# Residual add and layer norm: sums moved to GpSimd, and transfers of 16 rows split into even and odd partitions

## The chip, the cores and the metric

The kernel runs on one core of a Trainium2 chip. A core has five engines that run side by side: TensorE (PE, matrix products), VectorE (DVE), ScalarE (ACT), GpSimd (POOL) and SyncE (SP), which here only issues transfers. Sixteen DMA engines move data between the chip's memory (HBM) and the on-chip buffer SBUF (128 partitions). PSUM is a second, small on-chip buffer of eight banks, into which TensorE writes its results. The metric is device time in microseconds (us), the median of several runs; smaller is better.

## The reference

Input are `x` and `residual`, both 16 x 1024 x 512 in fp32, and `gamma` and `beta` of 512 elements. Each of the 16384 rows is normalized by itself:

```python
z = x + residual
mean = np.mean(z, axis=-1, keepdims=True)
var = np.var(z, axis=-1, keepdims=True)
z_norm = (z - mean) / np.sqrt(var + eps)
return (gamma * z_norm + beta).astype(np.float32)
```

The two inputs are 33.5 MB each, and so is the output: 100.7 MB cross the DMA engines.

## The kernel before

**Tiling.** The 16384 rows are laid over 128 partitions, so each partition has 128 rows of 512 elements; "row j" below means one such row in every partition, a tile of 128x512. `dram` (L58) cuts the input and output in blocks of the store sizes (`OUT_CHUNKS`: seven of 16 rows, then 8, 4, 4); in a block a partition owns as many neighbouring rows of HBM as the block has, so a 16-row store is one run of 32 KB per partition and an 8-row load one run of 16 KB.

**Buffers.** `zbuf` holds 64 rows of x, which become the sum, then the result, in place. `rbuf` holds 32 rows of the residual. Both are rings.

**Transfers.** All are issued by SyncE, in the order in which the last loop of the kernel asks for them: 8 rows of x (L81), 8 rows of the residual (L84), and a store (L87) when `STORE_LAG` = 40 rows more have been asked for than the store's last row. SyncE's queue is in order: a transfer that must wait holds back all behind it. A load of x waits until the store of the rows whose place it takes has landed. A load of the residual waits until the sums of the rows 32 before it are done. A store waits until its rows are finished. The DMA engines serve the issued transfers in order.

**Compute.** It goes by groups of four rows. A group passes through these stages, in three successive steps, so that three groups are under way at once:

1. `add` (L132, L133): TensorE multiplies the row of x, then the row of the residual, by an identity matrix into one PSUM bank, which adds them. Of every eight rows the last is left to VectorE (`add_on_vector`, L140).
2. `copy_then_sqrt` (L156): ScalarE copies the sum from PSUM to `zbuf` and gives the row's total; it also takes the root of the variance of an older group (L197). `negmean` (L171): VectorE turns the totals into negative means.
3. `square` (L185): ScalarE squares the centred row into a scratch tile in SBUF, for the sum of squares.
4. `affine1` (L209): VectorE adds the negative mean and multiplies by gamma. `affine2` (L222, L224): it takes the reciprocal of the root, multiplies by it and adds beta. Both work in place.

Gamma and beta are spread over the partitions at the start by a product with a column of ones (`spread`, L115) and copied to SBUF (L116). The program writes the order of the work on each engine out by hand (`manual_schedule`); the framework only adds the waits.

Of the kernel before, what the change touches and what calls it, by code (L numbers as in the profile page):

```python
# [7 lines left out]

FP32 = mybir.dt.float32
ACT = mybir.ActivationFunctionType  # L10
ALU = mybir.AluOpType

X_CHUNKS = [8] * 15 + [4, 4]
R_CHUNKS = [8] * 15 + [4, 4]
OUT_CHUNKS = [16] * 7 + [8, 4, 4]

GROUP = 4

Z_ROWS = 64
R_ROWS = 32

STORE_LAG = 40

ADD_PERIOD = 8


@with_exitstack
def kernel(  # L30
# [9 lines left out]
    nc = tc.nc  # L40
    P = nc.NUM_PARTITIONS
    xf = x.flatten_outer_dims()
    rf = residual.flatten_outer_dims()
    of = out.flatten_outer_dims()
    N, D = xf.shape
    inv_d = 1.0 / float(D)
    total = N // P

    def spans(sizes):

        assert sum(sizes) == total
        return [(sum(sizes[:c]), n) for c, n in enumerate(sizes)]

    blocks = spans(OUT_CHUNKS)

    def dram(t, lo, n):  # L58

        b0, bn = next(b for b in blocks if b[0] <= lo and lo + n <= b[0] + b[1])  # L60
        v = t[P * b0 : P * (b0 + bn), :].rearrange("(p j) d -> p j d", p=P)
        return v[:, lo - b0 : lo - b0 + n, :].rearrange("p a b -> p (a b)")

    consts = ctx.enter_context(tc.tile_pool(name="consts", bufs=1))
    small = ctx.enter_context(tc.tile_pool(name="small", bufs=6))
    junkp = ctx.enter_context(tc.tile_pool(name="junkp", bufs=2))
    psum = ctx.enter_context(
        tc.tile_pool(name="psum", bufs=8, space=bass.MemoryType.PSUM)
    )
    ctx.enter_context(tc.manual_schedule())  # L70

# [1 line left out]
    zbuf = consts.tile([P, Z_ROWS, D], FP32)  # L73
    rbuf = consts.tile([P, R_ROWS, D], FP32)

    def part(buf, size, lo, n):
        assert lo % size + n <= size
        return buf[:, lo % size : lo % size + n, :].rearrange("p a b -> p (a b)")

    def load_x(lo, n):  # L80
        nc.sync.dma_start(out=part(zbuf, Z_ROWS, lo, n), in_=dram(xf, lo, n))  # L81

    def load_r(lo, n):
        nc.sync.dma_start(out=part(rbuf, R_ROWS, lo, n), in_=dram(rf, lo, n))  # L84

    def store(lo, n):
        nc.sync.dma_start(out=dram(of, lo, n), in_=part(zbuf, Z_ROWS, lo, n))  # L87

    def zrow(j):
        return zbuf[:, j % Z_ROWS, :]  # L90

    def rrow(j):
        return rbuf[:, j % R_ROWS, :]

    def on_vector(j):
        return j % ADD_PERIOD == ADD_PERIOD - 1

    gb_row = consts.tile([1, 2, D], FP32)  # L100
    nc.scalar.dma_start(out=gb_row[:, 0, :], in_=gamma[None, :])
    nc.scalar.dma_start(out=gb_row[:, 1, :], in_=beta[None, :])
    ones = consts.tile([1, P], FP32)
    nc.vector.memset(ones, 1.0)  # L104
    eps_t = consts.tile([P, 1], FP32)
    nc.vector.memset(eps_t, float(eps))
    ident = consts.tile([P, P], FP32)
    make_identity(nc, ident)
    gamma_t = consts.tile([P, D], FP32)
    beta_t = consts.tile([P, D], FP32)  # L110

    def spread():
        for k, dest in ((0, gamma_t), (1, beta_t)):
            ps = psum.tile([P, D], FP32, tag="ps", name="ps")
            nc.tensor.matmul(ps, ones, gb_row[:, k, :], start=True, stop=True)  # L115
            nc.vector.tensor_copy(dest, ps)  # L116

    groups = []
    for lo, n in spans(R_CHUNKS):
        for j in range(0, n, GROUP):  # L120
            groups.append((lo + j, min(GROUP, n - j)))
    n_groups = len(groups)
    PS, SM, NM, SSQ, STD = {}, {}, {}, {}, {}

    def add(g):
        j0, n = groups[g]
        SM[g] = small.tile([P, GROUP], FP32, tag="sm", name="sm")
        for j in range(j0, j0 + n):
            if on_vector(j):
                continue  # L130
            ps = psum.tile([P, D], FP32, tag="ps", name="ps")
            nc.tensor.matmul(ps, ident, zrow(j), start=True, stop=False)  # L132
            nc.tensor.matmul(ps, ident, rrow(j), start=False, stop=True)  # L133
            PS[j] = ps

    def add_on_vector(g):
        j0, n = groups[g]
        for j in range(j0, j0 + n):
            if on_vector(j):
                nc.vector.scalar_tensor_tensor(  # L140
                    out=zrow(j),
                    in0=zrow(j),
                    scalar=0.0,
                    in1=rrow(j),
                    op0=ALU.add,
                    op1=ALU.add,
                    accum_out=SM[g][:, j - j0 : j - j0 + 1],
                )

    def copy_then_sqrt(g):  # L150

        j0, n = groups[g] if g < n_groups else (0, 0)
        before = g - 2 if g >= 2 else None
        for j in range(j0, j0 + n):
            if j in PS:
                nc.scalar.activation(  # L156
                    out=zrow(j),
                    in_=PS.pop(j),
                    func=ACT.Identity,
                    accum_out=SM[g][:, j - j0 : j - j0 + 1],  # L160
                )
                if before is not None:
                    sqrt(before)
                    before = None
        if before is not None:
            sqrt(before)

    def negmean(g):
        n = groups[g][1]
        nm = small.tile([P, GROUP], FP32, tag="nm", name="nm")  # L170
        nc.vector.tensor_scalar(  # L171
            out=nm[:, :n],
            in0=SM.pop(g)[:, :n],
            scalar1=-inv_d,
            scalar2=None,
            op0=ALU.mult,
        )
        NM[g] = nm

    def square(g):  # L180
        j0, n = groups[g]
        ssq = small.tile([P, GROUP], FP32, tag="ssq", name="ssq")
        for k in range(n):
            junk = junkp.tile([P, D], FP32, tag="junk", name="junk")
            nc.scalar.activation(  # L185
                out=junk,
                in_=zrow(j0 + k),
                func=ACT.Square,
                bias=NM[g][:, k : k + 1],
                accum_out=ssq[:, k : k + 1],  # L190
            )
        SSQ[g] = ssq

    def sqrt(g):
        n = groups[g][1]
        std = small.tile([P, GROUP], FP32, tag="std", name="std")
        nc.scalar.activation(  # L197
            out=std[:, :n],
            in_=SSQ.pop(g)[:, :n],
            func=ACT.Sqrt,  # L200
            bias=eps_t[:, 0:1],
            scale=inv_d,
        )
        STD[g] = std

    def affine1(g):
        j0, n = groups[g]
        for k in range(n):
            nc.vector.scalar_tensor_tensor(  # L209
                out=zrow(j0 + k),  # L210
                in0=zrow(j0 + k),
                scalar=NM[g][:, k : k + 1],
                in1=gamma_t,
                op0=ALU.add,
                op1=ALU.mult,
            )
        NM.pop(g)

    def affine2(g):
        j0, n = groups[g]  # L220
        rstd = small.tile([P, GROUP], FP32, tag="rstd", name="rstd")
        nc.vector.reciprocal(out=rstd[:, :n], in_=STD.pop(g)[:, :n])  # L222
        for k in range(n):
            nc.vector.scalar_tensor_tensor(  # L224
                out=zrow(j0 + k),
                in0=zrow(j0 + k),
                scalar=rstd[:, k : k + 1],
                in1=beta_t,
                op0=ALU.mult,
                op1=ALU.add,  # L230
            )

    def compute_steps():

        stages = [
            (0, add),
            (0, copy_then_sqrt),
            (1, square),
            (2, affine2),
            (0, add_on_vector),  # L240
            (1, affine1),
            (0, negmean),
        ]
        added = done = 0
        for t in range(n_groups + 2):
            for lag, stage in stages:
                if 0 <= t - lag < n_groups or stage is copy_then_sqrt:
                    stage(t - lag)
            if t < n_groups:
                added += groups[t][1]  # L250
            if t >= 2:
                done += groups[t - 2][1]
            yield added, done

    steps = compute_steps()
    added = done = asked = 0
    loads_r = spans(R_CHUNKS)
    stores = spans(OUT_CHUNKS)
# [10 lines left out]

    for lo, n in spans(X_CHUNKS):  # L270
        asked = lo + n
        assert not stores or stores[0][0] >= asked - Z_ROWS
        load_x(lo, n)
        while loads_r and loads_r[0][0] + loads_r[0][1] <= asked:

            while added < loads_r[0][0] + loads_r[0][1] - R_ROWS:
                added, done = next(steps)
# [39 lines left out]
```

## Time and profile before

| | |
|---|---|
| Median of 10 runs | 242.79 us (242.38 to 243.36) |
| The profiled execution's own time | 243.22 us |
| Its span (first to last instruction) | 241.3 us |
| TensorE matmul busy | 203.3 us (84%) |
| VectorE busy | 192.7 us (80%) |
| ScalarE busy | 169.9 us (70%) |
| GpSimd busy | 0.7 us |
| Moved | 100.79 MB, 418 GB/s on average |

How to read it: "busy" is the time in which an engine runs at least one instruction, and says nothing of whether it is waited for. A page has the busy share of every engine in 40 equal slices of the span, as tenths; a 9 means 90% or more. The row of DMA is the mean over the 16 DMA engines. A group line gives the source line, engine, operation, output and inputs, shape, count, busy time in all and the mean of one in nanoseconds. A timeline line gives start and duration in us, then engine, line and operation; "x4" means four in a row. SPq is SyncE's queue, in which the issue of a transfer appears; the transfer itself is in the DMA rows. "q1" is the queue of the loads and stores, "q8" and "q14" are queues on which instructions are fetched.

### The profile page before, as it was taken

Reading aid. Unit: us, or ns where it says so; the run is one execution under the profiler, and the core shown is the slowest. Engines: PE = TensorE matmul, PEld = TensorE weight load, DVE = VectorE, ACT = ScalarE, POOL = GpSimd, SP = SyncE. Lnnn points to the kernel's source line nnn. Section 1 sums busy time; section 2 is a strip of 40 time slices with the busy share of each in tenths; the row PEclk is TensorE's granted clock in tenths of the full one; section 3 lists DMA queues with packets and bytes.
Section 4 is the critical chain, followed back from the end, with each engine's and each line's share of the span. In section 5 each row is a group of like instructions: output and inputs, shape, how many; then the busy total and the mean of one; then the engine's idle time right before and its main releaser. Section 6 shows DMA issues by size and latency. Waiting matters only on the chain.

```text
span 241.3 us, 1990 instructions
## 1 busy us (share of the span) xinstructions
PE 203.3 (84%) x452; PEld 87.6 (36%) x452; DVE 192.7 (80%) x356; ACT 169.9 (70%) x514; POOL 0.7 (0%) x6
## 2 busy tenths in 40 slices
PE   3689999999999999999999996899959999891000
PEld 0134444444444444444444442344414444340000
DVE  1101279999999999999999999739997699989940
ACT  0213699797979797979797979269783888786500
POOL 1000000000000000000000000000000000000000
PEclk9999999999999999999999999799999999997555
DMA  7999999999999999999999999999999999999993
GB/s 261 435 435 435 432 427 424 417 427 431 435 465 435 388 428 421 435 429 427 428 432 437 436 424 429 424 451 418 416 432 432 469 391 414 462 426 435 410 414 148
DMA packets 6351, 100.79 MB, mean 418 GB/s; under 512 B 706, under 2 KB 706, under 8 KB 708
## 3 DMA queue, kind: packets, MB, share of 16 engines
q1 hardware_dynamic: 6336, 100.67, 98.0%
q8 instruction: 4, 0.07, 0.1%
q14 instruction: 7, 0.06, 0.1%
q10 hardware_dynamic: 4, 0.00, 0.0%
HBM read 67.11 MB, written 33.55 MB: 417 GB/s over the span
## 4 chain that ended last, share of the span: by engine, by line
PE 53%; DMA 34%; DVE 7%; SPq 1%; ACT 1%; issue 0%; DVEq 0%
DMA rbuf<-in_residual_dram 34%; PE ps L133 27%; PE ps L132 26%; DVE zbuf L209 3%; DVE zbuf L224 3%; SPq L81 0%; ACT junk L185 0%; ACT zbuf L156 0%; DVEq L312 0%; DVE zbuf L140 0%; SPq L87 0%; DVE rstd L222 0%; SPq L84 0%; DVE nm L171 0%; DVEq L209 0%
## 5 line engine op out<-in xcount | busy, mean ns | idle before, releaser
L133 PE MATMUL ps<-rbuf,ident 128*128 128x512 f32 x224 | 117.5, 607 | 9.9 <-DMA rbuf<-in_residual_dram 6.7
L132 PE MATMUL ps<-zbuf,ident 128*128 128x512 f32 x224 | 117.7, 607 | 0.0
L209 DVE SCALAR_TENSOR_TENSOR zbuf<-zbuf,nm,gamma_t 128x512 f32<-128x512 f32 x128 | 89.5, 749 | 12.6 <-ACT junk L185 12.6
L156 ACT ACTIVATE zbuf<-ps 128x512 f32<-128x512 f32 x112 | 66.0, 589 | 46.9 <-PE ps L133 46.9
L185 ACT ACTIVATE junk<-zbuf,nm 128x512 f32<-128x512 f32 x128 | 90.4, 711 | 1.6 <-DVE nm L171 1.6
L224 DVE SCALAR_TENSOR_TENSOR zbuf<-zbuf,rstd,beta_t 128x512 f32<-128x512 f32 x128 | 87.7, 748 | 1.1
L133 PEld LDWEIGHTS ps<-rbuf,ident 128*128 128x128 f32 x224 | 43.0, 194 | 67.0 <-issue 53.0
L132 PEld LDWEIGHTS ps<-zbuf,ident 128*128 128x128 f32 x224 | 43.6, 195 | 56.3 <-issue 43.1
L185 ACT ACTIVATION_READ_ACCUMULATOR junk<-zbuf,nm 128x1 f32 x128 | 24.3, 190 | 0.0
L156 ACT ACTIVATION_READ_ACCUMULATOR zbuf<-ps 128x1 f32 x112 | 21.8, 195 | 0.0
L171 DVE TENSOR_SCALAR nm<-sm 128x4 f32<-128x4 f32 x32 | 5.2, 163 | 13.6 <-ACT zbuf L156 13.6
L140 DVE SCALAR_TENSOR_TENSOR zbuf<-zbuf,rbuf 128x512 f32<-128x512 f32 x16 | 11.0, 686 | 0.0
L197 ACT ACTIVATE std<-ssq,eps_t 128x4 f32<-128x4 f32 x32 | 9.3, 289 | 0.1
L222 DVE RECIPROCAL rstd<-std 128x4 f32<-128x4 f32 x32 | 5.6, 174 | 3.8 <-ACT std L197 3.8
L115 PE MATMUL ps<-gb_row,ones 1*128 1x512 f32 x4 | 4.1, 1129 | 4.6 <-DMA gb_row<-in_gamma_dram 2.4
L156 ACT ACT_TABLE_LOAD x1 | 1.3, 1283 | 8.1 <-DMA zbuf<-in_x_dram 8.1
L116 DVE COPY beta_t<-ps 128x512 f32<-128x512 f32 x1 | 0.7, 692 | 3.6 <-PE ps L115 3.6
L116 DVE COPY gamma_t<-ps 128x512 f32<-128x512 f32 x1 | 0.7, 692 | 3.5 <-PE ps L115 3.5
L115 PEld LDWEIGHTS ps<-gb_row,ones 1*128 1x128 f32 x4 | 1.0, 307 | 6.1 <-DMA gb_row<-in_beta_dram 3.8
L140 DVE DVE_READ_ACCUMULATOR zbuf<-zbuf,rbuf 128x1 f32 x16 | 1.3, 83 | 0.0
L197 ACT ACT_TABLE_LOAD x1 | 1.3, 1283 | 0.0
L104 DVE MEMSET ones<- 1x128 f32 x1 | 0.2, 165 | 0.8 <-PEq L298 0.8
(7 smaller groups left out, 1.0 us busy)
## 6 DMA issues: line engine op xcount, KB each, us to landing
zbuf<-in_x_dram SPq DMA_DIRECT2D x15, 2048.0 KB, 25.2
rbuf<-in_residual_dram SPq DMA_DIRECT2D x15, 2048.0 KB, 20.8
out_dram<-zbuf SPq DMA_DIRECT2D x7, 4096.0 KB, 28.7
zbuf<-in_x_dram SPq DMA_DIRECT2D x2, 1024.0 KB, 33.1
rbuf<-in_residual_dram SPq DMA_DIRECT2D x2, 1024.0 KB, 33.1
out_dram<-zbuf SPq DMA_DIRECT2D x1, 2048.0 KB, 15.5
out_dram<-zbuf SPq DMA_DIRECT2D x2, 1024.0 KB, 10.2
gb_row<-in_gamma_dram ACTq DMA_DIRECT2D x1, 2.0 KB
```

The source lines that it names most:

```text
L115: nc.tensor.matmul(ps, ones, gb_row[:, k, :], start=True, stop=True)
L116: nc.vector.tensor_copy(dest, ps)
L132: nc.tensor.matmul(ps, ident, zrow(j), start=True, stop=False)
L133: nc.tensor.matmul(ps, ident, rrow(j), start=False, stop=True)
L140: nc.vector.scalar_tensor_tensor(out=zrow(j), in0=zrow(j), scalar=0.0, in1=rrow(j), op0=ALU.add, op1=ALU.add, accum_out=SM[g][:, j - j0 : ...
L156: nc.scalar.activation(out=zrow(j), in_=PS.pop(j), func=ACT.Identity, accum_out=SM[g][:, j - j0 : j - j0 + 1],)
L171: nc.vector.tensor_scalar(out=nm[:, :n], in0=SM.pop(g)[:, :n], scalar1=-inv_d, scalar2=None, op0=ALU.mult,)
L185: nc.scalar.activation(out=junk, in_=zrow(j0 + k), func=ACT.Square, bias=NM[g][:, k : k + 1], accum_out=ssq[:, k : k + 1],)
L197: nc.scalar.activation(out=std[:, :n], in_=SSQ.pop(g)[:, :n], func=ACT.Sqrt, bias=eps_t[:, 0:1], scale=inv_d,)
L209: nc.vector.scalar_tensor_tensor(out=zrow(j0 + k), in0=zrow(j0 + k), scalar=NM[g][:, k : k + 1], in1=gamma_t, op0=ALU.add, op1=ALU.mult,)
L222: nc.vector.reciprocal(out=rstd[:, :n], in_=STD.pop(g)[:, :n])
L224: nc.vector.scalar_tensor_tensor(out=zrow(j0 + k), in0=zrow(j0 + k), scalar=rstd[:, k : k + 1], in1=beta_t, op0=ALU.mult, op1=ALU.add,)
```

## The change

It has two steps that come together.

First, the arithmetic is moved. GpSimd adds a whole group in one instruction, in place in `zbuf`. ScalarE runs both statistics passes from `zbuf` into scratch tiles in PSUM: an Identity with scale -1/512, whose accumulator gives the negative mean directly, then the Square, then the root, whose result is in PSUM too. TensorE only spreads gamma and beta, which stay in PSUM, where VectorE's affine instructions read them. The stages of a group are issued one after the other with no lag between groups; the table of ScalarE's root function is loaded at the start by a small instruction (`warm`).

Second, loads of x are of 16 rows, loads of the residual of 8, 8, six times 16, 8, 4, 4, and blocks in HBM are always of 16 rows. A transfer of 16 rows is issued as two, one of the even and one of the odd partitions, 2 MB each with runs of 32 KB.

```diff
-X_CHUNKS = [8] * 15 + [4, 4]
-R_CHUNKS = [8] * 15 + [4, 4]
+BLOCK = 16
+X_CHUNKS = [16] * 8
+R_CHUNKS = [8, 8] + [16] * 6 + [8, 4, 4]
 OUT_CHUNKS = [16] * 7 + [8, 4, 4]
-ADD_PERIOD = 8
...
     def dram(t, lo, n):
-        b0, bn = next(b for b in blocks if b[0] <= lo and lo + n <= b[0] + b[1])
-        v = t[P * b0 : P * (b0 + bn), :].rearrange("(p j) d -> p j d", p=P)
-        return v[:, lo - b0 : lo - b0 + n, :].rearrange("p a b -> p (a b)")
+        k = lo % BLOCK
+        v = t[P * (lo - k) : P * (lo - k + BLOCK), :].rearrange("(p j) d -> p j d", p=P)
+        return v[:, k : k + n, :].rearrange("p a b -> p (a b)")
...
+    def transfer(out, in_, n):
+        parts = 2 if n == BLOCK else 1
+        for h in range(parts):
+            nc.sync.dma_start(out=out[h::parts, :], in_=in_[h::parts, :])
     def load_x(lo, n):
-        nc.sync.dma_start(out=part(zbuf, Z_ROWS, lo, n), in_=dram(xf, lo, n))
+        transfer(part(zbuf, Z_ROWS, lo, n), dram(xf, lo, n), n)
...
     def add(g):
         j0, n = groups[g]
+        z = part(zbuf, Z_ROWS, j0, n)
+        nc.gpsimd.tensor_tensor(
+            out=z, in0=z, in1=part(rbuf, R_ROWS, j0, n), op=ALU.add
+        )
...
+    def statistics(g):
+        j0, n = groups[g]
+        nm = small.tile([P, GROUP], FP32, tag="nm", name="nm")
+        ssq = small.tile([P, GROUP], FP32, tag="ssq", name="ssq")
+        for k in range(n):
+            junk = junkp.tile([P, D], FP32, tag="junk", name="junk")
+            nc.scalar.activation(
+                out=junk,
+                in_=zrow(j0 + k),
+                func=ACT.Identity,
+                scale=-inv_d,
+                accum_out=nm[:, k : k + 1],
+            )
+        for k in range(n):
+            junk = junkp.tile([P, D], FP32, tag="junk", name="junk")
+            nc.scalar.activation(
+                out=junk,
+                in_=zrow(j0 + k),
+                func=ACT.Square,
+                bias=nm[:, k : k + 1],
+                accum_out=ssq[:, k : k + 1],
+            )
+        std = stdp.tile([P, GROUP], FP32, tag="std", name="std")
+        nc.scalar.activation(
+            out=std[:, :n],
+            in_=ssq[:, :n],
+            func=ACT.Sqrt,
+            bias=eps_t[:, 0:1],
+            scale=inv_d,
+        )
...
+    gamma_t = fixed.tile([P, D], FP32, name="gamma_t")
+    beta_t = fixed.tile([P, D], FP32, name="beta_t")
...
+        for g in range(n_groups):
+            add(g)
+            statistics(g)
+            affine1(g)
+            affine2(g)
```

`fixed`, `junkp` (three buffers) and `stdp` (three) are pools in PSUM. `affine1` and `affine2` are as before but for the place of gamma and beta. The identity matrix, `add_on_vector`, `copy_then_sqrt` and `negmean` are gone.

## The prediction

> **What bounds the kernel now.** I read the page of the profiled execution first, the busy shares and the slices before anything else.
>
> ```profile
> span 241.3 us, 1990 instructions
> PE 203.3 (84%) x452; PEld 87.6 (36%) x452; DVE 192.7 (80%) x356; ACT 169.9 (70%) x514; POOL 0.7 (0%) x6
> ...
> DMA  7999999999999999999999999999999999999993
> ...
> q1 hardware_dynamic: 6336, 100.67, 98.0%
> q8 instruction: 4, 0.07, 0.1%
> q14 instruction: 7, 0.06, 0.1%
> ```
>
> TensorE is the busiest engine and fills half of the chain that ended last, but the DMA row is full from the second slice to the last but one, and the queue of loads and stores takes 98.0% of 16 engines' span. The transfers bound this kernel; the chain runs through TensorE because matmuls follow each other while the loads wait in a full queue. The tail says the same. In the timeline of SyncE and VectorE near the end:
>
> ```profile
> 181.19 50.81 SPq L87 DMA_DIRECT2D out_dram<-zbuf  x5
> ...
> 228.90 2.74 DVE L224 SCALAR_TENSOR_TENSOR zbuf<-zbuf,rstd,beta_t 128x512 f32<-128x512 f32 x4
> ```
>
> The last arithmetic ends at 231.6, and the stores still run to 240.2. The last store (8 packets of 0.309 an engine) has its place at 237.7 and needs 1.3 from issue to first packet, so compute had nearly 5 us to spare.
>
> So I went to the trace's record of each DMA packet. The median packet of 16 KB takes 0.611 us, of 32 KB 1.213, of 8 KB 0.309; a completion write takes 0.009. Each of the 16 engines carries 248, 56 and 48 of them (3968, 896 and 768 in all): 151.5 + 67.9 + 14.8 = 234.3, with 44 completion writes 234.7. The first packet starts at 2.0, so an undisturbed engine ends at 236.7. The last completion writes of the 16 engines lie at 236.71 (the first engine), within 0.3 of that for half of them, and at 237.7 to 240.17 for the other half. The span ends 1.1 later. So the time is 2.0 + 234.7 + 3.5 (the slowest engine's lateness) + 1.1 = 241.3. The profiled execution took 243.22, 1.92 outside the span; the median of the runs is 242.79, 0.43 less.
>
> What makes an engine late? Between 45 and 52 us, while two instruction fetches run (8 KB at 45.4 in 0.31 us, 16 KB at 47.5 in 1.10), the slowest engine's lateness goes from 0.4 to 1.9. By the first store, at 71, it is 2.8, with no fetch of its own there. The four 16 KB fetches (row q8) take 1.04 us on average.
>
> **What the skill says.** "Runtime: NRT & Kernel Launch", section Instruction fetch mechanics: instructions stream in 16 KiB blocks of 256, over DMA. This agrees with row q8: TensorE's 904 instructions are 3.5 blocks, and there are four such packets. "GPSIMD Engine Reference", section Performance versus the Vector engine: an add of two fp32 tensors with 2048 elements a partition takes 4497 ns on GpSimd. No row here shows one. "SBUF — State Buffer", section Who interferes with whom: a VectorE instruction with one SBUF input, outside the two-port modes, does not contend with GpSimd, one with two SBUF inputs does. Before, GpSimd is idle, so the trace can't say. "DMA: Bandwidth & Descriptors", section The descriptor swizzle: in a 128-partition transfer the engine is 8*(partition >> 6) + ((partition >> 2) & 7), each engine on one SBUF port. The even partitions give each engine four of its eight, if the rule holds for a step of two, which no run here shows.
>
> **The change, part by part.**
>
> **Bytes and packets.** The bytes stay. Loads of x, six of r and seven stores are now of 16 rows: (8 + 6 + 7) x 8 = 168 packets of 32 KB an engine. Three 8-row loads of r and one such store give 32 of 16 KB, four 4-row transfers 32 of 8 KB. 203.8 + 19.6 + 9.9 = 233.2, and 50 completion writes 0.45. That is 233.7 against 234.7: -1.0. Bounds: 0 if a 32 KB read costs two of 16 KB (only stores had 32 KB packets), -1.0 as here; I take -1.0.
>
> **Instruction fetch.** TensorE falls from 904 instructions to a handful, so the four 16 KB fetches go. ACT keeps about its number (256 activations with their accumulator reads), VectorE loses its 16 adds and 32 small scalings, so fetches of 8 KB (0.31 each) stay. Lateness between 0.4 (the spread in the first transfers) and 3.5 (unchanged). I take 1.5: two 16 KB fetches less, near 2 us, if the slowest engine had two of the four. That is -2.0, with bounds 0 and -3.1.
>
> **Adds on GpSimd.** 32 of 128x2048 at 4.5: 144 in all, 18 per 16 rows. A block of 16 rows takes 19.4 of DMA time while only loads run (2 MB take 4.86 in the first transfers) and 29.1 with its store. Hidden. What queues behind it: r of rows 32-47 waits for the adds of 0-15, r of 48-63 for those of 16-31, and on SP's queue everything behind. In the second case r of 16-31 lands at 41.2 (2.0 + 8 x 4.86 + 0.4), its adds end at 59.2, and the transfer's place in the DMA queue comes at 69.9, less 1.3 from issue to first packet (0.74 to 2.00 at the start): 9.4 to spare. An add may take up to 6.8. Without that cover each extra us of an add costs 4 per block.
>
> **ACT.** A row is now an Identity pass and a Square, both into PSUM. The timeline of ACT gives the pitch:
>
> ```profile
> 121.10 0.71 ACT L185 ACTIVATE junk<-zbuf,nm 128x512 f32<-128x512 f32 x1
> 121.72 0.19 ACT L185 ACTIVATION_READ_ACCUMULATOR junk<-zbuf,nm 128x1 f32 x1
> 121.81 0.58 ACT L156 ACTIVATE zbuf<-ps 128x512 f32<-128x512 f32 x1
> 122.29 0.19 ACT L156 ACTIVATION_READ_ACCUMULATOR zbuf<-ps 128x1 f32 x1
> 122.38 0.29 ACT L197 ACTIVATE std<-ssq,eps_t 128x4 f32<-128x4 f32 x1
> ```
>
> A Square takes 0.71 from start to start with its accumulator read, an Identity 0.57. Four rows: between 4 x 1.28 + 0.3 = 5.4 and, with the Identity at a Square's price and a stall before the root, 6.1. I take 5.6, so 22.4 a block, under 29.1. The first four blocks lag behind the loads, but their stores come long after: block 0 ends on VectorE near 48 and its store's place is at 79.6. The table load moves into the start (1.28, off the path).
>
> **VectorE.** Four affine instructions take 2.74 (the row above), so a group is 2.74 + 0.2 + 2.74 = 5.7, a block 22.8. Gamma and beta from PSUM: 0 to +0.1 each, hidden under 29.1. The copies of 0.69 from PSUM say near 0.
>
> **Shorter cover for the reuse of zbuf.** x of rows 64-79 now follows the store of 0-15 with nothing between; before, 8 rows of x and r (9.7) lay between. Each half waits for its own half of the store, so the other half, 4.86, covers the turn: the landing at 83.53 released an issue at 83.65, and 1.3 to the first packet makes 1.4. To spare: 3.4, at each of eight halves. Cost 0; with a turn of t above 4.86, 8 x (t - 4.86).
>
> **The tail.** Four blocks of stores are asked for after the last load, 38.8 of DMA time. With an end at 237.2 the last load lands at 198.4, r of 112-119 at 193.6. First add to 198.1, four ACT groups to 220.5, last VectorE work at 224.1. The last store's place is at 234.8: 9 to spare.
>
> **Sum.** 241.3 - 1.0 - 2.0 = 238.3 for the span, 240.2 for a profiled execution, 242.79 - 3.0 = 239.8 us for the median.
>
> **Rivals.** (1) No gain: packets of 32 KB read no faster and the lateness stays, because it comes from elsewhere (0.9 of it did, at 71): 242.8. (2) The other side: GpSimd's adds and VectorE exclude each other, although gamma lies in PSUM. The place is the affine stage; a block costs 22.8 + 18 = 40.8 instead of 29.1, in all 8 x 40.8 + 17 (first load) + 6 = 349. A milder form, adds of 9 us, gives 32 x 9 + 17 + 12 = 317. It decides from 6.8 per add. For: both use SBUF in every cycle; against: one SBUF input each. (3) Even and odd halves spread badly over the ports: two engines take turns on one port and 168 packets take double, +204, some 444. Against: the rule above. (4) The turn takes longer than 4.86; at 7 it is +17, 260. Against: the 0.12 above.
>
> **How the numbers follow.** About 0.2%, 0.5 us, is what a measurement here can tell from no change. Forecast 0.80, own range 238.2 to 242.0 (lateness 0.4 to 3.5, a little of the packets). Rival 1 0.07; rival 2 0.07; rival 3 0.04; rival 4 0.02. Faster 0.80, same 0.07, slower 0.13. The range 238.0 to 243.6 takes in the forecast and rival 1, and leaves out the 0.13 above.
>
> **What would show it.** DMA at 9 in all slices but the first and last; row q8 gone; GpSimd near 144 busy with 4.5 an add, none above 6.8; 32 KB loads at 1.21; VectorE near 0.75 an affine; the last engine's completion within 2 us of the first. I am wrong if a slice in mid-span falls below 9, if SP waits for GpSimd with an empty queue, or if affine instructions stretch while an add runs.

## The result, and the profile after

The kernel after takes 246.33 us in the median of 8 runs (245.71 to 246.74), against 242.86 in the runs of the kernel before beside it: a ratio of 1.014, with an interval of 1.0129 to 1.015. It is slower by 3.5 us where 3.0 less was forecast. The profiled execution took 246.74 us. Its page, cut to the rows that answer to those of before (busy shares, the 40 slices, the queues):

```profile
span 245.0 us, 1105 instructions
...
PE 4.1 (2%) x4; PEld 1.0 (0%) x4; DVE 178.4 (73%) x290; ACT 180.2 (74%) x546; POOL 143.8 (59%) x36
...
DMA  6999999999999999999999999999999999999993
GB/s 258 428 428 428 428 428 435 460 449 429 439 428 385 392 428 417 428 423 428 428 397 433 392 433 417 359 433 423 429 428 423 417 388 437 433 433 425 412 416 151
...
q1 hardware_dynamic: 4512, 100.67, 97.6%
q14 instruction: 9, 0.07, 0.1%
```

TensorE is gone as a consumer, row q8 has disappeared, GpSimd is busy for 143.8 us. The row of DMA is the one forecast, a 9 in every slice but the first and the last. By that row nothing is wrong. The row under it says more: the rate has dips to 385, 397, 392, 359, 388 GB/s in slices whose busy share is still 9. The engines are busy there, but slower. A single low slice is no proof yet, for a packet counts whole in the slice in which it starts. The row of before has two as well, 388 and 391, but each stands right behind a peak, 465 and 469, which makes up for it:

```profile
GB/s 261 435 435 435 432 427 424 417 427 431 435 465 435 388 428 421 435 429 427 428 432 437 436 424 429 424 451 418 416 432 432 469 391 414 462 426 435 410 414 148
```

The dips of after have no such peaks beside them.

The arithmetic came out as priced. The costliest groups (line, engine, operation, tiles, shapes and count, then busy us and mean ns of one, then the idle time before it):

```profile
L125 POOL TENSOR_TENSOR zbuf<-zbuf,rbuf 128x2048 f32<-128x2048 f32 x32 | 143.6, 4522 | 72.0 <-DMA rbuf<-in_residual_dram 56.8
L166 DVE SCALAR_TENSOR_TENSOR zbuf<-zbuf,nm,gamma_t 128x512 f32<-128x512 f32 x128 | 89.3, 746 | 48.1 <-ACT junk L145 25.1
L136 ACT ACTIVATE junk<-zbuf 128x512 f32<-128x512 f32 x128 | 74.3, 580 | 42.5 <-POOL zbuf L125 42.5
L180 DVE SCALAR_TENSOR_TENSOR zbuf<-zbuf,rstd,beta_t 128x512 f32<-128x512 f32 x128 | 87.1, 743 | 1.2
L145 ACT ACTIVATE junk<-zbuf,nm 128x512 f32<-128x512 f32 x128 | 85.8, 671 | 0.0
```

An add takes 4.52 us, none over 4.56, and the affine instructions 0.746 and 0.743 while GpSimd adds beside them: the two do not hold each other up. The tail, in the timeline of SyncE and VectorE:

```profile
185.54 43.38 SPq L86 DMA_DIRECT2D out_dram<-zbuf  x9
...
225.80 2.72 DVE L180 SCALAR_TENSOR_TENSOR zbuf<-zbuf,rstd,beta_t 128x512 f32<-128x512 f32 x4
```

The last arithmetic ends at 228.5 and the last store is issued at 228.9, while the stores run to 243.3. So the time is in the transfers, and in stretches of full busy shares. The windows of busy time around four of the dips (start and end in us; length; busy time of PE, PEld, DVE, ACT, POOL; granted clock; busy share of DMA; GB/s):

```profile
78.00:81.00 3.00, 0.00 (x0) 0.00 (x0) 3.00 (x6) 2.97 (x9) 2.74 (x1) 1.00 1.05 350
95.00:99.00 4.00, 0.00 (x0) 0.00 (x0) 3.96 (x7) 3.97 (x13) 4.00 (x2) 1.00 0.96 360
155.00:161.00 6.00, 0.00 (x0) 0.00 (x0) 5.96 (x11) 5.97 (x20) 6.00 (x2) 1.00 0.99 377
199.00:203.00 4.00, 0.00 (x0) 0.00 (x0) 3.96 (x8) 2.04 (x7) 4.00 (x2) 1.00 1.10 383
```

A share a little over 1 comes from the counting at the start of a packet and is to be read as full. What the reader is to see is the pair of the last two columns: share 0.96 to 1.10, rate 350 to 383. The rate divided by the share is free of that counting: 333, 375, 381 and 348 GB/s, where 428 to 433 is normal. The trace's record of each packet shows the same from the other end. A 32 KB packet has a median of 1.213 us, as forecast, but a mean of 1.240, a 99th percentile of 1.84 and a longest of 2.64. Call *excess* what all packets took over the median of their size, divided by the 16 engines, and *idle* the gaps between packets, per engine. The records do not name a packet's engine, so idle is good to some 0.2 us; a transfer ends with one small completion write from each engine, from which the ends are read:

| | before | after |
|---|---|---|
| first packet starts | 1.76 | 2.10 |
| excess over the span | 1.79 | 5.46 |
| idle over the span | 0.59 | 0.88 |
| first engine ends | 236.48 | 240.49 |
| last engine ends | 239.94 | 243.34 |
| span ends | 241.3 | 245.0 |

The excess of after lies in clusters of about 3 us, in which most of the 16 engines have a slow packet or two. There are two kinds of place. One is the reuse of `zbuf`: loads of x directly behind the store whose place they take (95.4 to 98.4, 0.50 an engine; 125.4 to 128.3, 0.32; 155.4 to 159.8, 0.70). The fourth reuse, near 186, has only 0.08, though nothing else lies behind its store either. The other is the last loads ahead of a store (78.0 to 80.6, 0.74; 107.6 to 110, 0.34; 137.6 to 141, 0.53; 168.3 to 170.9, 0.25; 198.7 to 202.2, 0.84). Before, apart from the first packets of all (0.65), no cluster is over 0.08.

The timeline of SyncE's queue in the kernel after shows what the two have in common:

```profile
60.89 1.11 SPq L86 DMA_DIRECT2D rbuf<-in_residual_dram  x2
62.10 1.18 SPq L86 DMA_DIRECT2D out_dram<-zbuf  x2
88.00 5.36 SPq L86 DMA_DIRECT2D zbuf<-in_x_dram  x2
93.46 1.19 SPq L86 DMA_DIRECT2D rbuf<-in_residual_dram  x2
94.74 1.19 SPq L86 DMA_DIRECT2D out_dram<-zbuf  x2
117.83 5.36 SPq L86 DMA_DIRECT2D zbuf<-in_x_dram  x2
```

From 63 to 88 SyncE can issue nothing, because the load of x waits for the store of 62.10 to land. The DMA engines work off the residual, then the store, and the store is the last thing in their queue. At 88.00, when the first half of the store has been finished by all engines (87.65), the first half of the load is issued, and only the second half of the store is left as *cover*. Such a reuse of a place is called a turn below. This repeats four times; up to the last turn a store is always the end of the queue. In the kernel before, the first load of x that reuses a place, at 83.65, finds more in the queue, for a load of x and one of the residual had been issued behind the store of 54.60:

```profile
55.07 0.59 SPq L81 DMA_DIRECT2D zbuf<-in_x_dram  x1
66.24 0.33 SPq L84 DMA_DIRECT2D rbuf<-in_residual_dram  x1
83.65 0.33 SPq L81 DMA_DIRECT2D zbuf<-in_x_dram  x1
```

The table of issues shows the depth of the queue over the whole run, in the median us from issue to landing. Of after:

```profile
zbuf<-in_x_dram SPq DMA_DIRECT2D x16, 2048.0 KB, 10.2
```

and of before:

```profile
zbuf<-in_x_dram SPq DMA_DIRECT2D x15, 2048.0 KB, 25.2
```

Both have the load's own 4.9 us in them. At the turns alone the difference is smaller: 14.6 before (issued at 83.65, landed at 98.26) and 9.7 after (88.00 and 97.66), as the cover is 9.7 and 4.9.

### The profile page after: what moved, and what is told of

It is laid out like the page before. It is cut to its first block, busy times and chain, and to the rows that moved or that the text cites. A ratio compares the mean times of both kernels' runs of the same rounds, so it can differ in the third digit from the quotient of the medians.

```text
span 245.0 us, 1105 instructions
## 1 busy us (share of the span) xinstructions
PE 4.1 (2%) x4; PEld 1.0 (0%) x4; DVE 178.4 (73%) x290; ACT 180.2 (74%) x546; POOL 143.8 (59%) x36
## 4 chain that ended last, share of the span: by engine, by line
DMA 69%; POOL 9%; DVE 7%; SPq 4%; POOLq 3%; issue 2%; DVEq 0%
DMA out_dram<-zbuf 46%; DMA rbuf<-in_residual_dram 20%; POOL zbuf L125 9%; SPq L86 4%; DVE zbuf L166 3%; DMA zbuf<-in_x_dram 3%; POOLq L266 3%; DVE zbuf L180 3%; DVEq L266 0%; DVE rstd L178 0%; POOLq L125 0%
## 5 line engine op out<-in xcount | busy, mean ns | idle before, releaser
L125 POOL TENSOR_TENSOR zbuf<-zbuf,rbuf 128x2048 f32<-128x2048 f32 x32 | 143.6, 4522 | 72.0 <-DMA rbuf<-in_residual_dram 56.8
L136 ACT ACTIVATE junk<-zbuf 128x512 f32<-128x512 f32 x128 | 74.3, 580 | 42.5 <-POOL zbuf L125 42.5
L145 ACT ACTIVATE junk<-zbuf,nm 128x512 f32<-128x512 f32 x128 | 85.8, 671 | 0.0
L136 ACT ACTIVATION_READ_ACCUMULATOR junk<-zbuf 128x1 f32 x128 | 23.9, 187 | 0.0
L153 ACT ACTIVATE std<-ssq,eps_t 128x4 f32<-128x4 f32 x32 | 8.6, 267 | 1.0
L195 PE MATMUL beta_t<-gb_row,ones 1*128 1x512 f32 x2 | 2.1, 1136 | 1.5 <-DMA gb_row<-in_beta_dram 1.5
L195 PE MATMUL gamma_t<-gb_row,ones 1*128 1x512 f32 x2 | 2.0, 1122 | 2.1 <-DMA gb_row<-in_gamma_dram 2.1
L195 PEld LDWEIGHTS beta_t<-gb_row,ones 1*128 1x128 f32 x2 | 0.5, 306 | 3.1 <-DMA gb_row<-in_beta_dram 3.1
L195 PEld LDWEIGHTS gamma_t<-gb_row,ones 1*128 1x128 f32 x2 | 0.5, 308 | 2.1 <-issue 2.1
## 6 DMA issues: line engine op xcount, KB each, us to landing
zbuf<-in_x_dram SPq DMA_DIRECT2D x16, 2048.0 KB, 10.2
```

The source lines that it names most:

```text
L125: nc.gpsimd.tensor_tensor(out=z, in0=z, in1=part(rbuf, R_ROWS, j0, n), op=ALU.add)
L136: nc.scalar.activation(out=junk, in_=zrow(j0 + k), func=ACT.Identity, scale=-inv_d, accum_out=nm[:, k : k + 1],)
L145: nc.scalar.activation(out=junk, in_=zrow(j0 + k), func=ACT.Square, bias=nm[:, k : k + 1], accum_out=ssq[:, k : k + 1],)
L153: nc.scalar.activation(out=std[:, :n], in_=ssq[:, :n], func=ACT.Sqrt, bias=eps_t[:, 0:1], scale=inv_d,)
L195: nc.tensor.matmul(dest, ones, gb_row[:, k, :], start=True, stop=True)
```

## The experiments

The theory formed from this: the short cover, and nothing of the arithmetic, is what costs; an excess of packets stands where the forecast had nothing. The rivals: the arithmetic (GpSimd, ScalarE and VectorE use SBUF while packets pass); the halves of 64 partitions by themselves; packets of 32 KB; and each change from loads to stores, whatever the cover. The diffs are against the kernel after unless another is named. "Over before" is the median less that of the kernel before run beside it.

### E1 and E2: one half of the change alone

E1 has the new arithmetic with the transfers of before:

```diff
-X_CHUNKS = [16] * 8
-R_CHUNKS = [8, 8] + [16] * 6 + [8, 4, 4]
+X_CHUNKS = [8] * 15 + [4, 4]
+R_CHUNKS = [8] * 15 + [4, 4]
...
-        parts = 2 if n == BLOCK else 1
-        for h in range(parts):
-            nc.sync.dma_start(out=out[h::parts, :], in_=in_[h::parts, :])
+        nc.sync.dma_start(out=out, in_=in_)
```

> The first step alone: the new arithmetic with the transfers of before (8-row loads, whole stores). My theory, that the transfers in halves cost the time: the packets keep their pace, TensorE's four instruction fetches are gone, 240 to 242 us, a little under before, slow 32 KB packets gone. Rival, that the new arithmetic's use of SBUF slows the packets: 245 to 246, slow packets remain.

E2 has the arithmetic of before with the transfers of after (the diff is against before):

```diff
+    def transfer(out, in_, n):
+        parts = 2 if n == BLOCK else 1
+        for h in range(parts):
+            nc.sync.dma_start(out=out[h::parts, :], in_=in_[h::parts, :])
...
-        nc.sync.dma_start(out=part(zbuf, Z_ROWS, lo, n), in_=dram(xf, lo, n))
+        transfer(part(zbuf, Z_ROWS, lo, n), dram(xf, lo, n), n)
```

> The second step alone: the arithmetic of before with the transfers of after. My theory (transfers in halves): 246 to 248, with the same slow packets at the reuse of zbuf and before each store. Rival (arithmetic): 241.5 to 243.

E1: 243.23 us, 1.0013 (1.0006 to 1.0019), 0.25 over before. E2: 248.96, 1.0235 (1.0198 to 1.0272), 5.98 over before. The page of E1:

```profile
span 242.0 us, 1109 instructions
...
DMA  7999999999999999999999999999999999999991
GB/s 263 433 431 433 433 432 431 428 432 417 420 466 435 390 433 433 466 428 393 432 431 463 402 428 425 420 444 425 424 431 436 441 416 414 460 429 429 422 416 66
...
q1 hardware_dynamic: 6336, 100.67, 97.6%
q14 instruction: 9, 0.07, 0.1%
```

All 32 adds of GpSimd, all statistics of ScalarE, no q8, and the excess is 1.60, as before (1.79). The arithmetic falls as a rival. It also gives nothing, where 240 to 242 was expected, though the 16 KB fetches are gone: fourteen engines end by 237.9 (239.0 before), but two end at 240.0 and 240.4, later than the last one before (239.9). E2 has slow packets at the same kinds of place with TensorE doing the sums: an excess of 7.44, and an idle of 2.99 besides. The loss is in the transfers. It is larger with the old arithmetic than with the new, so the two steps of the change do not simply add.

### E3: halves by rows instead of by partitions

```diff
-            nc.sync.dma_start(out=out[h::parts, :], in_=in_[h::parts, :])
+            w = n // parts * 512
+            nc.sync.dma_start(
+                out=out[:, h * w : (h + 1) * w], in_=in_[:, h * w : (h + 1) * w]
+            )
```

> As after, but a transfer of 16 rows is cut into two of 8 rows over all 128 partitions, so packets are of 16 KB and the order of the transfers and what covers each reuse stay. If the short cover alone costs the time: 246 still. If the halves of partitions (or reads of 32 KB) cost it all: 241 to 242. If both, as I think: 243 to 244.5, with slow packets left at the reuse and none before the stores.

244.78 us, 1.0072 (1.0058 to 1.0085), 1.80 over before. The order of the transfers and the cover are as in after, but packets are of 16 KB over 128 partitions. The excess is 3.65, with clusters at the third and fourth turn (0.86 from 149 to 159, 0.24 from 184 to 189) and at later changes from loads to stores (0.09, 0.26, 0.12 and 0.58, where none was expected), and none at the first change. The loss is about halved: it needs neither halves of the partitions nor 32 KB packets, but it grows with the two together.

### E4, E5 and E6: cover and halves, one at a time

E4 asks for a store ahead of the residual of its round, so that the load that reuses its place has the residual, of 9.7 us, as cover:

```diff
     load_x(lo, n)
+    if asked < total:
+        store_due()
     while loads_r and loads_r[0][0] + loads_r[0][1] <= asked:
```

> As after, but a store is asked for ahead of the residual of the same turn and not behind it, so 9.7 us of loads lie between a store and the load that takes its place. If the short cover costs about 1.8 us, as I think: 244 to 245, slow packets left only where a load is followed by a store. If the cover costs nothing: 246. If it costs all: 242 to 243.

E5 is E4 with whole transfers of 16 rows over 128 partitions:

```diff
-        parts = 2 if n == BLOCK else 1
+        parts = 1
```

> As e4_early (stores asked for ahead of the residual, 9.7 us of cover), but a transfer of 16 rows is one transfer over all 128 partitions, still of 32 KB packets. If the halves of partitions cost the rest (the 0.8 us at the first change from loads to stores and the later first packet): 243 to 243.5, and no slow packets there. If reads of 32 KB cost it: 244.5 as e4_early, slow packets there as in it.

E6 is after with the same whole transfers: a load of x then waits for a whole store with nothing behind it, a cover of zero.

> As after, but whole transfers of 16 rows: a load of x then waits for the store just ahead of it with nothing behind, so each of the four turns stands bare in the DMA rows. By the step of my prediction (1.4 us a turn): four gaps of 1.4, some 247 us. If a turn really takes about 3 us from landing to full pace, which would explain slow packets under a cover of 4.85 less the 2 us by which engines differ: four gaps of 2.5 to 3.5, 251 to 254 us.

| | us | ratio (interval) | over before | excess | idle |
|---|---|---|---|---|---|
| after: halves, short cover | 246.33 | 1.0140 (1.0129 to 1.0150) | 3.47 | 5.46 | 0.88 |
| E4: halves, long cover | 244.48 | 1.0059 (1.0045 to 1.0073) | 1.50 | 2.00 | 1.37 |
| E5: whole, long cover | 243.40 | 1.0019 (1.0011 to 1.0026) | 0.37 | 1.91 | 1.76 |
| E6: whole, no cover | 256.74 | 1.0564 (1.0549 to 1.0578) | 13.71 | 8.22 | 10.3 |

In E4 the order at the turn is x, store, residual, and the load of x goes out 10 us earlier against its store. The timeline of SyncE's queue in E4:

```profile
78.34 5.32 SPq L86 DMA_DIRECT2D zbuf<-in_x_dram  x2
83.75 1.19 SPq L86 DMA_DIRECT2D out_dram<-zbuf  x2
84.99 1.23 SPq L86 DMA_DIRECT2D rbuf<-in_residual_dram  x2
107.90 5.29 SPq L86 DMA_DIRECT2D zbuf<-in_x_dram  x2
```

and its windows, at the first change from loads to stores, and at the first and the third turn:

```profile
68.00:72.00 4.00, 0.00 (x0) 0.00 (x0) 3.96 (x8) 3.97 (x14) 4.00 (x2) 1.00 1.08 377
88.00:98.00 10.00, 0.00 (x0) 0.00 (x0) 7.75 (x13) 4.76 (x15) 4.88 (x2) 1.00 0.98 423
148.00:158.00 10.00, 0.00 (x0) 0.00 (x0) 5.14 (x9) 2.54 (x8) 5.44 (x2) 1.00 1.02 439
```

The turns are at full rate. Of the clusters only the start (0.63) and the first change (0.84) are left, and the excess falls from 5.46 to 2.00. The change of order is worth 2.0 us of the median, and part of it is lost again in the tail: E4's arithmetic ends at 234.4 instead of 228.5, and the stores wait for it (GB/s 335 in the last but one slice, idle 1.37). E5 takes off another 1.1: the first packet starts at 1.75 instead of 2.10, and SyncE needs 0.4 us for 16 rows instead of 1.2. E5 also keeps the cluster at the first change (0.69), which was expected to go with the halves, so that one does not come from them.

E6 shows the bare turn. Its page:

```profile
DMA  8999999999999949999699995999978999999996
GB/s 309 398 434 437 462 428 411 432 457 417 416 437 397 457 159 447 411 355 462 253 411 428 396 406 252 411 411 411 407 334 324 411 420 402 416 432 459 423 399 263
```

and its queue of SyncE at the first of the four turns:

```profile
60.96 0.43 SPq L86 DMA_DIRECT2D out_dram<-zbuf  x1
92.56 0.33 SPq L86 DMA_DIRECT2D zbuf<-in_x_dram  x1
93.01 0.36 SPq L86 DMA_DIRECT2D rbuf<-in_residual_dram  x1
```

Here the row of DMA does show the loss, as digits of 4, 6, 5 and 7. By the packet records the engines end the store between 90.06 and 92.22; 0.34 after the last of them the load is issued, its first packet starts 0.96 later, at 93.52, and the first packets of the 16 engines take 1.91 on average instead of 1.21. So a turn is 1.3 from the last engine's end to the first packet, 0.7 for a slow first packet, and ahead of that the 2.2 for which the first engine waits for the last (0.5 to 1.6 at the other three turns). The last loads ahead of each store are slow besides, with an excess of 0.47 at the first and 0.92 to 1.11 at the others, against 0.65 to 0.70 at each turn. The time is above both of the expected ones, which had counted a gap at each turn alone.

With these terms the cover of after can be read from its own packets. At its four turns the last engine ended the first half of the store at 87.65, 117.49, 148.14 and 178.15, and the engine that is furthest ahead ends the second half at 90.67, 120.29, 150.32 and 180.65: 3.0, 2.8, 2.2 and 2.5 later, not 4.85, because the engines have drifted apart by 1.8 to 2.7. Less 1.3 for the start, 0.9 to 1.7 is to spare (0.2 to 1.0 with a slow first packet), not 3.4.

### E7: loads of the residual of 8 rows, in E5

```diff
-R_CHUNKS = [8, 8] + [16] * 6 + [8, 4, 4]
+R_CHUNKS = [8] * 15 + [4, 4]
```

> As e5_whole_early, but the residual in loads of 8 rows, so that the last sums can begin 4.9 us earlier and the last stores don't wait for arithmetic. If cover and halves were the whole loss: 242 to 242.8, as before or a little under. If something else of the new transfers costs time: 243.5 or more.

243.58 us, 1.0022 (1.0014 to 1.0030), level with E5. The idle falls (0.37) and the cluster at the first change shrinks to 0.25, but the last engine still ends 3.3 after the first (239.41 against 236.10). The profiled execution, 243.01, was the fastest of the thirteen. By what was expected, 243.5 or more means that cover and halves were not the whole loss: 0.55 is left without them.

### E8 and E9: one turn at a time

E8 is E4, but the last turn has the order of after, with its short cover:

```diff
     load_x(lo, n)
+    if asked < total - BLOCK:
+        store_due()
```

E9 is after, but the last turn has the order of E4; the same two lines stand there with `asked == total - BLOCK` as the condition.

> As e4_early, but the last reuse alone (rows 48-63 stored, then x of 112-127) keeps the short cover of after. If a tight turn also costs at the next change from loads to stores, some 15 us later (four stores stand in the queue by then in e4_early and in after alike): slow 8 KB packets before the store of 64-79, 0.5 to 0.9 us an engine, with 0.2 to 0.9 at the turn itself, and 245 us. If that loss came from anything else that after has and e4_early lacks: none there, 0.2 to 0.9 at the turn only.

> The reverse: as after, but the last reuse alone has the long cover. If a tight turn costs at the next change: no slow packets before the store of 64-79, all others as in after, 245.3 us. If not: 0.8 us an engine there as in after, 246 us.

E8: 244.94, 1.0092 (1.0071 to 1.0112), 2.07 over before. E9: 245.26, 1.0104 (1.0086 to 1.0122), 2.39 over before. Against E4 (1.50) and after (3.47) one turn is worth 0.6 in E8 and 1.1 in E9, where an even share of the 2.0 over four turns would be 0.5. The windows of E8, at three places that are clean in E4 (there the last has 472 GB/s at a share of 1.11):

```profile
178.00:181.00 3.00, 0.00 (x0) 0.00 (x0) 2.96 (x6) 2.97 (x11) 3.00 (x1) 1.00 1.08 360
184.00:190.00 6.00, 0.00 (x0) 0.00 (x0) 5.96 (x10) 5.97 (x20) 6.00 (x2) 1.00 0.88 354
197.00:200.00 3.00, 0.00 (x0) 0.00 (x0) 2.96 (x7) 3.00 (x11) 3.00 (x1) 1.00 1.15 407
```

The second is the turn itself (excess 0.57), where after has next to nothing at the same turn (0.08): the same short cover does not cost the same each time. The first is the last loads ahead of the store that nothing follows (0.74); no short turn has come before it. The third is the change to the last four blocks of stores, after the short turn (0.61). In E9, where the last turn is the long one, the first and the third place have no cluster, while its earlier turns look as in after. So both kinds of cluster, at the turn and at the change from loads to stores, come and go with the short cover nearby.

### E10: the instruction fetches back

E1, and TensorE multiplies small tiles that nobody reads, so that it has as many instructions as before and their fetches again (the tile that they write takes PSUM from `stdp`, which has two buffers for three):

```diff
+    def idle_matmuls(g):
+        r = rrow(groups[g][0])
+        nc.tensor.matmul(spare[:1, :8], r[:, :1], r[:, :8], start=True, stop=True)
+        for k in range(6):
+            nc.tensor.matmul(
+                spare[:, :8], ones, gb_row[:, 0, :8], start=True, stop=True
+            )
```

> e1_arithmetic with 224 small products added on TensorE whose results nobody reads, so that TensorE again has some 900 instructions and fetches four blocks of 16 KB. Their work is hidden. If those fetches set the slowest engine, as the prediction said: 2 us over e1_arithmetic (243.2), some 245. If they only make more engines late and not the slowest later: within 0.5 of it, 243.2 to 243.7.

242.94 us, 0.9999 (0.9989 to 1.0010): level with before, and if anything below E1. The page of E10:

```profile
span 241.0 us, 2006 instructions
...
q8 instruction: 3, 0.05, 0.1%
```

Three fetches of 16 KB are back, where before had four, and the time is none the longer; the last engine ends 2.9 after the first, in E1 3.9. In the time the fetches cost nothing that this measurement can tell; what each does to one DMA engine is taken up below.

### E11 and E12: the whole queue deeper

E11 is after with stores 24 rows behind the loads instead of 40, so that a place is reused two blocks later:

```diff
-STORE_LAG = 40
+STORE_LAG = 24
```

> As after, with STORE_LAG 24 for 40: a store is asked for one block earlier, so a whole block of x and residual (19.4 us) lies between it and the load that takes its place, while each store still follows directly on loads of the residual and the next loads stand behind it. If the short cover makes both kinds of slow packets: none left but at the start and the first change, 244 to 245. If a change from loads of the residual to a store costs by itself: 0.3 to 0.7 us an engine at each, 245 to 246.

E12 is E11 with whole transfers, and the lag of 40 again from row 112 on, so that four blocks of stores remain for the end:

```diff
-        parts = 2 if n == BLOCK else 1
+        parts = 1
...
-            stores[0][0] + stores[0][1] <= asked - STORE_LAG or asked == total
+            stores[0][0] + stores[0][1] <= asked - (24 if asked < 112 else 40)
+            or asked == total
```

> As after, with transfers of 16 rows over all 128 partitions, and stores asked for 24 rows behind the loads until row 96, so that a place of zbuf is reused two blocks after its store is asked for; the blocks from row 64 on keep the lag of 40 and are stored at the end. Theory (cover of the reuse decides, halves cost about 1 us more): no slow packets but at the first change from loads to stores (0.6 to 0.7 an engine), first packet at 2.0, no idle time in mid-span; the first engine ends near 236.5 and the last 3 to 4 later, so a span of 240.7 to 241.7 and a median of 242.3 to 243.3, level with before. Rival (the halves cost nothing, what is gained comes from the lag alone): as with the lag of 24 and halves but for its tail, 243.0 to 243.8. Second rival (loss at every change from loads to stores whatever the cover): excess of 4 to 5 an engine, 245 to 246.

E11: 243.74, 1.0041 (1.0025 to 1.0057). One line of the schedule takes back 2.6 of the 3.5 us, with halves, 32 KB packets and the new arithmetic all in place. The page of E11, the row of the slices' rates and the first row of issues:

```profile
GB/s 261 434 409 458 434 434 435 434 428 429 379 434 434 435 428 428 434 434 434 434 434 434 424 434 429 434 434 428 434 434 435 434 409 417 454 434 434 416 305 182
...
zbuf<-in_x_dram SPq DMA_DIRECT2D x16, 2048.0 KB, 34.9
```

34.9 us from issue to landing instead of 10.2, and from the twelfth slice to the thirty-second the rate stays between 424 and 435. Stores still follow loads of the residual in mid-span, and after the first there is no cluster over 0.11: a change from loads to stores costs little or nothing by itself. What is left is the start (0.73), the first change (0.60, at 58 to 61), and the tail, where only three blocks of stores cover the last arithmetic (305 GB/s, idle 3.24 in all). E12: 243.72, 1.0033 (1.0017 to 1.0049). Its excess is 1.79 with the start (0.72) and the first change (0.52) in it, but it idles for 1.7 near the end, and the last engine is 2.8 late. That is above the 242.3 to 243.3 of the theory and inside the range of the first rival, that the halves cost nothing. The two tails differ, so E12 does not refute a cost of the halves, but it does not confirm it: with the deeper queue, taking the halves away gained nothing (0.92 over before, 0.87 in E11). No version was faster than the kernel before; E10 was level with it.

## Why the prediction was wrong, step by step

The forecast was 239.8 us and the measurement 246.33, outside the range and on the other side. The prediction gives the times of packets 0.24 us later than the packet records have them: its first packet at 2.00 starts at 1.76, its last completion at 240.17 is at 239.94. Its sums stand, but the 1.3 from the first issue to the first packet is 1.03, and the 0.12 from the landing to the next issue is 0.36. On the times of the records, the span was put at 238.3 and was 245.0, 6.7 more: the first engine ended at 240.5 instead of 235.5 (5.0), the last 2.85 after it instead of 1.5 (1.35), and the span 1.6 after that instead of 1.3 (0.3). By steps:

**Instruction fetch, -2.0: wrong.** The step took the last engine's lateness of 3.5 us to go with TensorE's four fetches of 16 KB, and priced the fetches of 8 KB that stay at their own 0.31. E1 takes TensorE's fetches away and ends 0.25 over before, E10 puts three back and ends level. The sentence of the Trainium skill that bears on the time stands in the very section that the prediction read ("Runtime: NRT & Kernel Launch", Instruction fetch mechanics): "The cost of crossing a 16 KiB boundary is one DMA tail-bump, mostly hidden." E10 agrees, as far as its time goes. The lateness is 2.6 to 3.9 without TensorE's fetches, in E1, E4, E5, E7 and E12, and 2.9 with three of them in E10. In E11 the engines end within 0.2 of each other, because there the last stores wait for the arithmetic, and that kernel is no faster for it.

That a fetch makes an engine late was read rightly, though. The completion writes show it as steps, counted here up to 190 us. In before and in E10 the lateness of all engines together grows by 1.5 to 2.3 us at each fetch of 16 KB, but the last engine moves only at the first one (0.74 to 1.87 and 0.71 to 1.89); the others fall to engines that are not the last. The fetches of 8 KB on queue q14 make an engine late by more than their 0.31. In E12 the last engine is 0.4 behind the first at 32 us, 1.1 at 41, 1.8 at 61, 2.6 at 90, 3.4 at 139 and 4.1 at 187: a step of 0.7 to 0.9 at each of five fetches (38.0, 61.4, 83.4, 134.2 and 183.2) and none between them. So the lateness comes back from the fetches that stay. This is read from the traces; no run takes these fetches away, and not every step has a fetch beside it (E1 has one of 1.1 between 95 and 100).

**Shorter cover for the reuse of `zbuf`, 0 with 3.4 to spare: wrong, and the larger miss.** The turn was put at 1.4 us, landing to first packet. E6 measures 1.3 for the same, and then two terms that the step left out: a first packet that is 0.7 longer, and the engines' drift, since a load waits for the last engine of the store while the first is already 1.8 to 2.7 into its cover. That leaves 0.9 to 1.7 of the 3.4, or 0.2 to 1.0 with the slow first packet. So even then the queue does not run dry, and these terms alone would still say that nothing is lost. The cost did not come in the form in which the prediction would have looked for it. It named a slice below 9; the slices stayed at 9, the idle grew by 0.3, and the packets got longer, by 3.7 an engine. Lengthening the cover alone takes back 2.0 (E4) or 2.6 (E11).

**Bytes and packets, -1.0: right in its own term, and paid back elsewhere.** The packets number as counted and their median is 1.213. But the halves cost 1.1 (E4 to E5; E11 to E12 does not show it), part of it the later first packet (2.10 for 1.75), and loads of 32 KB came with 0.5 to 0.8 at the first change in E4, E5, E8, E11 and E12, where loads of 16 KB had at most 0.10 (before, E1, E3). E5, with neither halves nor a short cover, ends 0.37 over before.

The miss of 6.5 adds up as 2.25 for the arithmetic (forecast -2.0, E1 +0.25) and 4.2 for the transfers (forecast -1.0, measured 3.47 - 0.25 = 3.2). Of the 3.2, about 2.0 is the cover and 1.1 the halves. This split holds for the order in which the parts are taken away here, from after to E4 to E5 and E1: in E2 the transfers alone cost 5.98, and in E11 the cover gives back 2.6.

**Adds on GpSimd, ACT, VectorE, the tail: right.** 4.52 against 4.5 an add, 5.6 a group on ScalarE as put (180.2 us in 32 groups), 0.746 and 0.743 an affine instruction against 0.75, the last VectorE work at 228.5 against 224.1, still more than 9 us ahead of its store's place (the first engine's last 2.5 us, from 238.0). Rival 2, GpSimd and VectorE excluding each other, is refuted by those rows, and rival 3, a bad spread of the halves over the ports, by the median of 1.213. Rival 4, the turn, had the right place and got 0.02 of the chance: it was priced as idle time that starts sharply at 4.86, and so looked harmless at 1.4. Rival 1's reason, a lateness that does not go with TensorE's fetches, held.

**Open.** Why packets lengthen when little is queued behind them, though the engines do not run dry, is not shown. That the short cover brings it about is (E4, E8, E9, E11); the mechanism below it is not, and a short cover does not do it every time (the last turn of after). Nor is it known why the first change from loads to stores loses 0.25 to 0.84 with 32 KB loads under any cover, whether the halves cost 1.1 in every schedule, nor why a fetch of 0.31 us holds its engine up by 0.7, and whether such fetches are all of the 2.6 to 3.9 us between the first and the last DMA engine.

## What to carry to other kernels

In a kernel bound by transfers a busy share of 9 is no proof of full speed: read the rate row beside it, leave out low slices that stand next to a peak, and take the windows of the slices in which the two part. When transfers are merged or reordered, work out for each buffer that is reused what still lies in the DMA queue between the store and the load into its place, and count the turn as landing to first packet, plus the slow first packet, plus the drift between the engines; keep well over that, since here the loss began before the queue ran dry. And before the cost of one source goes into a sum, ask what else makes the same cost: the last engine stayed late when TensorE's fetches were gone, because others remained.

## What the runs showed of the hardware that was not expected

- Packets take longer without idle time: 32 KB at 1.3 to 2.6 us instead of 1.213, on most of the 16 engines within about 3 us, at a turn with a short cover and on the last loads ahead of a store that nothing follows.
- A start from an empty queue costs 0.96 us from the start of the issue to the first packet (E6; 1.03 at the start of before) and 0.65 to 0.7 more in the first packets (E6, all four turns). "DMA: Bandwidth & Descriptors", section Specifications, of the Trainium skill has about 0.6 us to the first byte for this way of issuing. The packet records here agree if one counts from the end of the issue (92.89 to 93.52 in E6, 0.63); for the load the issue's own 0.33 comes on top.
- A transfer of 64 partitions with a step of two runs at full rate (a median of 1.213 us per 32 KB packet), but its issue takes about 0.6 us on SyncE (E4, 5 halves and more), against 0.33 to 0.43 for 128 partitions (E6), so that 16 rows cost SyncE three times as much.
- The DMA engines do not end together: the last is 3.5 us behind the first before, and 2.6 to 3.9 in E1, E4, E5, E7, E10 and E12, in E4 and E5 because of two of the sixteen (the records do not say which). A fetch of 8 KB, 0.31 us long, goes with 0.7 to 0.9 us more of it in E12.
